# A decoder layer on one core: matmul operands read from two halves in turn, results taken out of PSUM in token order

## The chip, the cores and the metric

The kernel runs on one core of a Trainium2 chip. A core has five engines with their own instruction streams. TensorE (PE in the profile; its weight loads are PEld) multiplies matrices and writes to PSUM. VectorE (DVE), ScalarE (ACT) and GpSimd (POOL) do elementwise work. SyncE (SP) issues the DMAs. Operands lie in SBUF, 128 partitions side by side; a tile here is 128 partitions by up to 1024 float32 values.

The metric is the device time in microseconds (us) of one execution. A profile is one execution, recorded by the hardware profiler.

## The reference

One layer of a hybrid decoder, 1024 tokens of width 1024, float32:

```python
z = rms_norm(h, norm_mix_g); proj = z @ w_in                  # 1024 -> 1536
y_pool = multiscale_pool_mixer(proj[..., :512], ...)          # windows 2, 4, 8, 16, then 4 blocks of 128x128
xb = causal_depthwise_conv(proj[..., 512:1024], ...)          # 4 taps
y_lru = rg_lru(xb, gates ...) * gelu(proj[..., 1024:])        # sigmoid gates (64x64 blocks), linear recurrence
h = h + concat(y_pool, y_lru) @ w_out
z = rms_norm(h, norm_mlp_g)
h = h + square(relu(z @ w_up)) @ w_down                       # 1024 -> 4096 -> 1024
z = rms_norm(h, norm_ple_g)
h = h + sigmoid(z @ w_ple_gate + b) * (p @ w_ple_proj)
out = rms_norm(h, norm_final_g)
```

## The kernel before

**Layout.** Everything is held with the features on the partitions and the tokens along the free dimension: `H[0..7]` are eight tiles of 128 features by 1024 tokens. `T` are six work tiles, `R` holds 1/rms for each token. A matmul takes a 128x128 block of weights as the stationary operand and streams up to 512 tokens (columns) of a tile as the moving operand. Its result, 128 features by 512 tokens, fills one PSUM bank.

**Precision.** Each product of two float32 values is made of three products of rounded values (the type float32r). `split` (lines 151 to 159) writes hi, the rounded copy, on ScalarE, and lo, the rest, on VectorE. `mm` (lines 311 to 329) multiplies hi by hi, hi by lo and lo by hi into the same bank; line 321 issues nearly all matmuls of the program. `lru_gates` issues its own (line 523), two of 64 rows side by side. The sums of squares for the norms multiply by a tile of ones: lines 385 and 386 with float32r operands, line 395 with plain float32. Ten matmuls on a tile of ones (line 428) stand ahead of the first data.

**Stages**, in the order of the program:

- the first projection (`ps_l`), three output tiles accumulated while the eight tiles of x arrive and are split;
- the other projections (`ps_i`, `project`), with convolution, pooling windows, gates (`ps_g`, sigmoid on ScalarE, line 531), pool products (`ps_p`, line 591) and scans between them; `normed` (line 488) multiplies each result by R as it takes it out of PSUM;
- the output projection (`ps_o`), added to `H` on line 632;
- the up product (`ps_P_u`). Tokens and features are cut into halves, and each 2x2 block product is computed with seven products instead of eight (`P1` to `P7`, a Strassen-Winograd scheme), 16 pairs of output tiles. `copy` (line 704, ScalarE) and `add` (line 672, VectorE) take each product out of PSUM and combine it. `P5` is added to both rows of a pair through `twice`. `finish_up` then does relu, R and square, and the result goes to DRAM;
- the down product (`ps_P_d`), the same scheme over two chunks of the hidden features, accumulated in `H` (line 672 again);
- the per-layer gate (`ps_e` and `ps_j`) in three token groups, 512, 256 and 256 (`GROUPS`). `ple_out` (lines 953 to 968) takes the gate out of PSUM on line 959 or 957 and the projection on line 965;
- the final norm, with the stores.

**What sets the order.** A scheduling layer orders the instructions of each engine by readiness and priority from the order in which the code issues them; `pin` and `tc.keep_in_program_order` hold some in place. PSUM has eight banks: four single ones (`pd`) and two tiles of two banks (`pp`). `psum` and `mlp_bank` hand them out in turn. A product can start when its bank has been emptied and its operands are split.

What a result in PSUM looks like in the kernel before: column n of the bank is token n of the half. All readers take it in one run of 512 (or 1024, or 256).

Of the kernel before, what the change touches and what calls it, by code (L numbers as in the profile page):

```python
# [9 lines left out]
AF = mybir.ActivationFunctionType  # L10
ALU = mybir.AluOpType

P = 128
# [3 lines left out]
HALF = 512  # L17
# [34 lines left out]
def block_kernel(  # L52
# [85 lines left out]

    def f32(ap):
        return ap.bitcast(F32)  # L140

    def col(name, i):
        c = COLS[name] + i
        return vecs[:, c : c + 1]
# [166 lines left out]
    def mm(parts, whi, wlo, zhi, zlo, first, last, only=None, more=False, held=False):  # L311
        outs = [
            (slice(hs.start + n, hs.start + min(n + HALF, w)), ps[:, n : min(n + HALF, w)])
            for hs, ps in parts
            for w in (hs.stop - hs.start,)
            for n in range(0, w, HALF)
            if only is None or hs.start + n == only.start
        ]
        for w, z in ((whi, zhi), (whi, zlo), (wlo, zhi)):
            for hs, ps in outs:  # L320
                ins = nc.tensor.matmul(  # L321
                    ps, w, z[:, hs],
                    start=first and z is zhi and w is whi,
                    stop=last and w is wlo,
                    skip_group_check=more,
                )
                if held:
                    tc.keep_in_program_order(ins)
                    held = False
# [155 lines left out]

    def normed(dst, parts):
        for hs, ps in parts:
            nc.vector.tensor_tensor(dst[:, hs], ps, R[:, hs], ALU.mult)

    def conv(o, ps):  # L490
        u, xb = (H[6], T[4])[o % 2], H[o]
# [17 lines left out]
    def lru_gates(o):  # L509


        hi, lo = hl(0), hl(2)
        ct, rt, _ = LSETS[o % 2]
        zhi, zlo = B[4 + o]
        ps = [psum(f"ps_g{h}{o}") for h in range(2)]
        halves = [
            [(hs.start + n, x[:, n : n + HALF]) for hs, x in parts for n in range(0, hs.stop - hs.start, HALF)]
            for parts in ps
        ]
        for n, (w, z) in enumerate(((hi, zhi), (hi, zlo), (lo, zhi))):  # L520
# [12 lines left out]
        return last.ins  # L533

# [48 lines left out]
    def pool_mix(pair):  # L583
        whi, wlo = hl(1), hl(3)
        for t in range(2):
            g = 2 * pair + t
            y = (T[5], T[2])[t]
            ps = psum(f"ps_p{g}")
            mm(ps, kblk(whi, g), kblk(wlo, g), *B[g], True, True)
            for hs, part in ps:  # L590
                nc.scalar.activation(
                    y[:, hs], part, AF.Identity, bias=pool_bs[:, g : g + 1], scale=col("pool_s", g)
                )
            split(y, *B[g])

# [75 lines left out]
    def add(to, x, y=None, eng=None):  # L671
        (eng or nc.vector).tensor_tensor(to, to if y is None else y, x, ALU.add)  # L672

    def twice(x):
        return x.unsqueeze(1).broadcast_to([P, 2, x.shape[-1]])

# [42 lines left out]
    def up_first():  # L719
        cc, c11, c12, c21, c22, s = up_sums(0)  # L720
        ps = {}
        ws = {}
        for kinds in (("P6", "P7"), ("P4", "P5")):
            for kind, w in zip(kinds, weights()):
                ws[kind] = w
                ps[kind] = mlp_bank(f"ps_{kind}_u0")
                product(ps[kind], w, lambda t, kind=kind: up_operand(kind, t), range(3))
        for kind in ("P6", "P7", "P4", "P5"):
            product(ps[kind], ws[kind], lambda t, kind=kind: up_operand(kind, t), range(3, 4))
        copy(s, ps["P5"])  # L730
# [9 lines left out]
        add(c12, ps["P6"], c11)  # L740
        add(c22, ps["P7"], c12)
        add(c11, ps["P2"])
        add(c21, ps["P4"], c22)
        add(c22, s)
        add(c12, ps["P5"])
        norm.rstd(R, parts)
        done.append((0, cc))

    def up_pair(m):
        cc, c11, c12, c21, c22, s = up_sums(m)  # L750

        def of(kind, w):
            ps = mlp_bank(f"ps_{kind}_u{m}")
            product(ps, w, lambda t: up_operand(kind, t))
            return ps
# [2 lines left out]
        if m == NPAIR - 1:  # L758
            preload_down()
        copy(s, of("P1", wa))  # L760
        add(c11, of("P2", wb), s)
        if m > 1:
            store_up = finish_up(*done.pop())
            if m < NPAIR - 1:
# [2 lines left out]
            leave("hl")  # L767
        wa, wb = weights()
        copy(c12, of("P3", wb))
        add(s, of("P6", wa))  # L770
# [4 lines left out]
        add(c22, of("P7", wa), s)  # L775
        if m == NPAIR - 1:
            ask()
            prepare(0, 0)
        add(c21, of("P4", wb), c22)
        if m == 1:  # L780
            finish_up(*done.pop())()
        wa, _ = weights()
# [55 lines left out]
    def down(n):  # L838
# [6 lines left out]
        for q in range(NQ):  # L845
# [17 lines left out]
                    load_w(0, ij, i)  # L863
            if kind == "P1":
                copy(u, x)
                add(c11, x)
            elif kind == "P2":
                add(c11, x)
            elif kind == "P6":
                add(u, x)  # L870
                add(c12, u, eng=None)
            elif kind == "P7":
                add(u, x)
                add(H[2 * q + 1].rearrange("p (y s) -> p y s", y=2), twice(u))
            elif kind == "P4":
                add(c21, x)
            elif kind == "P5":
                add(h_all[:, 2 * q : 2 * q + 2, SECOND], twice(x))
            else:
                add(c12, x)  # L880
            for tp in AHEAD[q] if n else AHEAD[q - 1]:
                prepare(n + 1, tp)
            if last:
# [69 lines left out]
    def ple_out(hs, o, pg, pj, add=True, then=None):  # L953
        t = T[3 + o % 2][:, : hs.stop - hs.start]
        hv = H[o][:, hs]
        if hs == GROUPS[-1]:
            pin(nc.scalar.activation(t, pg, AF.Sigmoid, bias=col("b_ple", o)))
# [172 lines left out]
```

## Time and profile before

| | us |
|---|---|
| median of 3 runs | 972.97 (972.44 to 973.43) |
| the profiled execution | 972.32 |
| its span, first to last instruction | 970.4 |
| TensorE busy | 960.2 |
| VectorE busy | 747.2 |
| ScalarE busy | 459.1 |
| GpSimd busy | 99.1 |

The granted clock of TensorE was 0.997 of full on the mean. How to read the views quoted below: a group of instructions is one row, with line, engine, operation, what it writes and reads by the program's names, shapes and count, then busy us, the mean ns of one, and the idle time of the engine before them with what ended it. Matmuls are pipelined: a record begins when the columns start to stream and ends when the last result is out, so records overlap, and the pace is read from start to start. A mean that is marked with other forms mixes shapes. "L321" is line 321 of the kernel; after the change the same statement stands on line 336.

### The profile page before, as it was taken

The page shows a single profiled execution, that of the slowest core. Times are in us where ns is not written, and L with a number is a line of the kernel's source. Part 1 is how long each engine was busy: PE and PEld are TensorE (multiplying, and loading weights), DVE is VectorE, ACT ScalarE, POOL GpSimd, SP SyncE. Part 2 cuts the span into 40 slices and gives each one's busy share as a digit, 9 for nine tenths or more (in the row PEclk, how much of TensorE's full clock was granted, in tenths as well). Part 3 has the DMA queues.
Part 4 walks back from the last instruction along what each step waited for, and adds up shares of the span by engine and source line. Part 5 has one row for each costly group of instructions (what it writes and reads, how often), then busy time and mean ns, then how long its engine had stood idle before and what let it go on. Part 6 is the DMA issues. An engine that isn't in the chain of part 4 may idle for free.

```text
span 970.4 us, 11500 instructions
## 1 busy us (share of the span) xinstructions
PE 960.2 (99%) x4472; PEld 800.1 (82%) x4472; DVE 747.2 (77%) x865; ACT 459.1 (47%) x546; POOL 99.1 (10%) x72
## 2 busy tenths in 40 slices
PE   9999999999999999999999999999999999999996
PEld 7888788888788888888888888888888888888996
DVE  7997965459887777777677889879675669784976
ACT  8368793347443343334334535443443346552635
POOL 0000000002523322322331000000000000000220
PEclk9999999999999999999999999999999999999998
DMA  7311133112154345344434997356532341031122
GB/s 254 95 44 44 46 130 129 44 43 72 59 169 168 120 162 193 123 133 167 179 119 141 325 367 253 109 190 208 179 105 87 109 152 44 10 122 44 44 88 87
DMA packets 45190, 125.04 MB, mean 129 GB/s; under 512 B 4176, under 2 KB 6224, under 8 KB 45136
## 3 DMA queue, kind: packets, MB, share of 16 engines
q1 hardware_dynamic: 44992, 124.27, 37.9%
q8 instruction: 35, 0.57, 0.2%
q14 instruction: 19, 0.16, 0.0%
q10 hardware_dynamic: 144, 0.04, 0.0%
HBM read 90.74 MB, written 33.55 MB: 128 GB/s over the span
## 4 chain that ended last, share of the span: by engine, by line
PE 95%; DVE 3%; ACT 1%; DMA 0%; issue 0%; SPq 0%; DVEq 0%
PE ps_P_d L321 31%; PE ps_P_u L321 31%; PE ps_i L321 10%; PE ps_o L321 9%; PE ps_e L321 8%; PE ps_l L321 3%; PE ps_j L321 1%; PE ps_g L523 1%; PE ps_p L321 1%; DVE h L981 1%; DMA h<-in_xT 0%; DVE a L155 0%; DVE a L158 0%; DVE t L997 0%; DVE wu_lo L155 0%
## 5 line engine op out<-in xcount | busy, mean ns | idle before, releaser
L321 PE MATMUL ps_P_d<-a,wd_P_hi 128*128 128x512 f32 x880 | 270.8, 389 | 0.0
L321 PEld LDWEIGHTS ps_P_d<-a,wd_P_hi 128*128 128x128 f32 x880 | 165.2, 188 | 34.3
L321 PE MATMUL ps_P_d<-a,wd_P_lo 128*128 128x512 f32 x440 | 171.2, 389 | 0.0
L321 PE MATMUL ps_P_u<-a,wu_hi 128*128 128x512 f32 x512 | 157.7, 389 | 0.0
L321 PE MATMUL ps_P_u<-y,wu_hi 128*128 128x512 f32 x384 | 118.1, 389 | 0.0
L321 PEld LDWEIGHTS ps_P_u<-a,wu_hi 128*128 128x128 f32 x512 | 96.1, 188 | 20.1
L321 PE MATMUL ps_P_u<-a,wu_lo 128*128 128x512 f32 x256 | 99.6, 389 | 0.0
L672 DVE TENSOR_TENSOR t<-t,ps_P_u 128x512 f32<-128x512 f32 (+1 forms) x80 | 62.6, 784 | 47.3 <-PE ps_P_u L321 47.1
L321 PEld LDWEIGHTS ps_P_d<-a,wd_P_lo 128*128 128x128 f32 x440 | 82.6, 188 | 17.2
L321 PEld LDWEIGHTS ps_P_u<-y,wu_hi 128*128 128x128 f32 x384 | 72.1, 188 | 15.0
L321 PE MATMUL ps_i<-a,wi_hi 128*128 128x512 f32 x288 | 77.5, 391 | 0.0
L321 PE MATMUL ps_P_u<-y,wu_lo 128*128 128x512 f32 x192 | 74.8, 390 | 0.4 <-DVE wu_lo L155 0.4
L155 DVE TENSOR_TENSOR a<-wd,a 128x1024 fp32r<-128x1024 f32 x56 | 67.1, 1219 | 4.5 <-ACT a L154 3.5
L154 ACT ACTIVATE a<-wd 128x1024 fp32r<-128x1024 f32 x56 | 58.9, 1057 | 22.3 <-DMA wd<-act 12.0
L321 PE MATMUL ps_o<-y,wo_hi 128*128 128x512 f32 x256 | 68.4, 389 | 0.0
L321 PEld LDWEIGHTS ps_i<-a,wi_hi 128*128 128x128 f32 x288 | 53.7, 188 | 12.4 <-issue 1.4
L154 ACT ACTIVATE wu_hi<-wu 128x1024 fp32r<-128x1024 f32 x24 | 25.5, 1063 | 78.2 <-PE ps_P_u L321 43.9
L154 ACT ACTIVATE wu_hi<-wu_raw 128x1024 fp32r<-128x1024 f32 (+1 forms) x25 | 25.3, 1011 | 78.0 <-PE ps_P_u L321 44.5
L321 PEld LDWEIGHTS ps_o<-y,wo_hi 128*128 128x128 f32 x256 | 48.0, 188 | 10.0
L321 PEld LDWEIGHTS ps_P_u<-a,wu_lo 128*128 128x128 f32 x256 | 48.0, 188 | 9.9
L154 ACT ACTIVATE wd_P_hi<-wd 128x1024 fp32r<-128x1024 f32 x24 | 25.4, 1060 | 56.5 <-PE ps_P_d L321 51.9
L155 POOL TENSOR_TENSOR wg_lo<-wg_raw,wg_hi 128x1024 fp32r<-128x1024 f32 x4 | 9.9, 2478 | 408.0 <-DVE h L966 381.4
(224 smaller groups left out, 1628.7 us busy)
## 6 DMA issues: line engine op xcount, KB each, us to landing
wd<-act SPq DMA_DIRECT2D x56, 512.0 KB, 5.5
act<-t SPq DMA_DIRECT2D x32, 512.0 KB, 4.6
wu_raw<-in_w_up SPq DMA_DIRECT2D x16, 512.0 KB, 3.2
wu<-in_w_up SPq DMA_DIRECT2D x16, 512.0 KB, 4.1
act<-wu SPq DMA_DIRECT2D x16, 512.0 KB, 5.1
wd<-in_w_down SPq DMA_DIRECT2D x16, 512.0 KB, 6.4
h<-in_xT SPq DMA_DIRECT2D x15, 512.0 KB, 4.5
wg_raw<-in_w_gate SPq DMA_DIRECT2D x12, 512.0 KB, 3.4
```

The costliest lines, as they stand in the source:

```text
L154: first = pin(nc.scalar.activation(hi, src, AF.Copy))
L155: pin((eng or nc.vector).tensor_tensor(lo, src, f32(hi), ALU.subtract))
L321: ins = nc.tensor.matmul(ps, w, z[:, hs], start=first and z is zhi and w is whi, stop=last and w is wlo, skip_group_check=more,)
L523: nc.tensor.matmul(x, w[r, o * P : (o + 1) * P], z[r, at : at + HALF], start=n == 0, stop=n == 2)
L672: (eng or nc.vector).tensor_tensor(to, to if y is None else y, x, ALU.add)
L981: nc.vector.scalar_tensor_tensor(hv, hv, col("g_fin", o), rfin[:, hs], ALU.mult, ALU.mult)
```

## The change

Three helpers are added. `turns(z)` reads a moving operand of 512 columns as 0, 256, 1, 257, ..., 255, 511 (one of 256 as 0, 128, 1, 129, ...). The bank is still written in one run, so its column 2j holds token j of the half and column 2j + 1 token j + 256. `got(ps)` reads a bank so that the tokens come out in order: 256 values with a step of two, then the 256 between them; of a tile of two banks it does so bank by bank. `by(x, ps)` gives a tile in SBUF the same shape, which leaves its addresses in one run.

All products on lines 321 and 523 read through `turns`. All readers of their banks use `got` and `by`: `normed`, the sigmoids of `lru_gates`, `pool_mix`, the residual add of the output projection, `copy`, the adds of the up and down products (`add_got`, and `add_both` for `P5`), and `ple_out`. The matmuls on a tile of ones (lines 385, 386, 395 and 428) and what reads their banks stay as they were. Weights, splits, DMAs and the arithmetic are untouched.

On every engine the instructions stand in the same order, with the same buffers, as before; only the access patterns of operands differ.

```diff
+    def turns(z):
+        return z.rearrange("p (a j) -> p j a", a=2)
+
+    def got(ps):
+        if ps.shape[-1] > HALF:
+            return ps.rearrange("p (b j a) -> p b a j", b=2, a=2)
+        return ps.rearrange("p (j a) -> p a j", a=2)
+
+    def by(x, ps):
+        if ps.shape[-1] > HALF:
+            return x.rearrange("p (b a j) -> p b a j", b=2, a=2)
+        return x.rearrange("p (a j) -> p a j", a=2)
...
                 ins = nc.tensor.matmul(
-                    ps, w, z[:, hs],
+                    ps, w, turns(z[:, hs]),
...
     def normed(dst, parts):
         for hs, ps in parts:
-            nc.vector.tensor_tensor(dst[:, hs], ps, R[:, hs], ALU.mult)
+            nc.vector.tensor_tensor(by(dst[:, hs], ps), got(ps), by(R[:, hs], ps), ALU.mult)
...
-                        x, w[r, o * P : (o + 1) * P], z[r, at : at + HALF], start=n == 0, stop=n == 2
+                        x, w[r, o * P : (o + 1) * P], turns(z[r, at : at + HALF]), start=n == 0, stop=n == 2
...
-                        last = nc.scalar.activation(dst[HEADS[h], hs], part[r], AF.Sigmoid, bias=col(b, o)[r])
+                        last = nc.scalar.activation(
+                            by(dst[HEADS[h], hs], part), got(part[r]), AF.Sigmoid, bias=col(b, o)[r]
+                        )
...
-            nc.vector.tensor_tensor(H[o][:, hs], H[o][:, hs], part, ALU.add)
+            hv = by(H[o][:, hs], part)
+            nc.vector.tensor_tensor(hv, hv, got(part), ALU.add)
...
+    def add_got(to, ps, y=None):
+
+        add(by(to, ps), got(ps), None if y is None else by(y, ps))
+
+    def add_both(to, ps):
+
+        to = to.rearrange("p c (a j) -> p c a j", a=2)
+        add(to, got(ps).unsqueeze(1).broadcast_to([P, 2, 2, ps.shape[-1] // 2]))
...
-    def copy(to, x):
-        nc.scalar.activation(to, x, AF.Copy)
+    def copy(to, ps):
+        nc.scalar.activation(by(to, ps), got(ps), AF.Copy)
...
-        add(c11, of("P2", wb), s)
+        add_got(c11, of("P2", wb), s)
...
-        add(cc[:, :, SECOND], twice(p5))
+        add_both(cc[:, :, SECOND], p5)
...
-            nc.vector.tensor_tensor(t, pg, R[:, hs], ALU.mult)
+            nc.vector.tensor_tensor(by(t, pg), got(pg), by(R[:, hs], pg), ALU.mult)
...
-        nc.vector.tensor_tensor(e, t, pj, ALU.mult)
+        nc.vector.tensor_tensor(by(e, pj), by(t, pj), got(pj), ALU.mult)
```

More of the change, by code (lines that the diff above doesn't have):

```diff
@@ L591, in pool_mix @@
                 nc.scalar.activation(
-                    y[:, hs], part, AF.Identity, bias=pool_bs[:, g : g + 1], scale=col("pool_s", g)
+                    by(y[:, hs], part), got(part), AF.Identity, bias=pool_bs[:, g : g + 1], scale=col("pool_s", g)
                 )
@@ L739, in up_first @@
         copy(c11, ps["P1"])
[L740 to L743, printed above, removed]
+        add_got(c12, ps["P6"], c11)
+        add_got(c22, ps["P7"], c12)
+        add_got(c11, ps["P2"])
+        add_got(c21, ps["P4"], c22)
         add(c22, s)
-        add(c12, ps["P5"])
+        add_got(c12, ps["P5"])
         norm.rstd(R, parts)
@@ L769, in up_pair @@
         copy(c12, of("P3", wb))
-        add(s, of("P6", wa))
+        add_got(s, of("P6", wa))
         wa, wb = weights()
@@ L774, in up_pair @@
                 store_up()
-        add(c22, of("P7", wa), s)
+        add_got(c22, of("P7", wa), s)
         if m == NPAIR - 1:
@@ L778, in up_pair @@
             prepare(0, 0)
-        add(c21, of("P4", wb), c22)
+        add_got(c21, of("P4", wb), c22)
         if m == 1:
@@ L865, in down @@
                 copy(u, x)
-                add(c11, x)
+                add_got(c11, x)
             elif kind == "P2":
-                add(c11, x)
+                add_got(c11, x)
             elif kind == "P6":
-                add(u, x)
-                add(c12, u, eng=None)
+                add_got(u, x)
+                add(c12, u)
             elif kind == "P7":
-                add(u, x)
+                add_got(u, x)
                 add(H[2 * q + 1].rearrange("p (y s) -> p y s", y=2), twice(u))
             elif kind == "P4":
-                add(c21, x)
+                add_got(c21, x)
             elif kind == "P5":
-                add(h_all[:, 2 * q : 2 * q + 2, SECOND], twice(x))
+                add_both(h_all[:, 2 * q : 2 * q + 2, SECOND], x)
             else:
-                add(c12, x)
+                add_got(c12, x)
             for tp in AHEAD[q] if n else AHEAD[q - 1]:
@@ L956, in ple_out @@
         if hs == GROUPS[-1]:
-            pin(nc.scalar.activation(t, pg, AF.Sigmoid, bias=col("b_ple", o)))
+            pin(nc.scalar.activation(by(t, pg), got(pg), AF.Sigmoid, bias=col("b_ple", o)))
         else:
-            nc.vector.tensor_tensor(t, pg, R[:, hs], ALU.mult)
+            nc.vector.tensor_tensor(by(t, pg), got(pg), by(R[:, hs], pg), ALU.mult)
             nc.scalar.activation(t, t, AF.Sigmoid, bias=col("b_ple", o))
```

## The prediction

> **What bounds the kernel now.** I read the page's busy times first, then the chain that ended last, then busy time by stage, then single matmuls in the timeline.
>
> ```profile
> span 970.4 us, 11500 instructions
> PE 960.2 (99%) x4472; PEld 800.1 (82%) x4472; DVE 747.2 (77%) x865; ACT 459.1 (47%) x546; POOL 99.1 (10%) x72
> PE 95%; DVE 3%; ACT 1%; DMA 0%; issue 0%; SPq 0%; DVEq 0%
> ```
>
> TensorE is busy in 960.2 of 970.4 us and holds 95% of the chain. Nothing but its own pace, and the few places where it waits, can move the end. The stages, cut by hand at the borders that the chain of waits shows (the columns are the stretch and its length, then busy us and instructions of PE, PEld, DVE, ACT and POOL, the granted clock, the DMA share and GB/s):
>
> ```profile
> 1.31:5.72 4.41, 4.41 (x11) 3.46 (x11) 1.41 (x6) 2.58 (x5) 0.00 (x0) 1.00 0.71 213
> 5.72:36.00 30.28, 29.98 (x132) 24.24 (x131) 26.86 (x55) 20.42 (x25) 0.00 (x0) 1.00 0.62 214
> 36.00:150.00 114.00, 114.00 (x521) 92.26 (x520) 97.82 (x102) 85.49 (x89) 0.00 (x0) 1.00 0.21 70
> 150.75:237.79 87.04, 87.04 (x385) 72.07 (x385) 54.12 (x61) 39.03 (x43) 5.68 (x3) 1.00 0.19 61
> 237.79:258.50 20.71, 20.26 (x89) 16.43 (x89) 19.85 (x24) 11.18 (x16) 7.83 (x4) 1.00 0.29 102
> 258.51:544.35 285.84, 285.84 (x1261) 236.37 (x1261) 215.89 (x216) 106.55 (x126) 75.50 (x58) 1.00 0.45 154
> 544.35:849.00 304.65, 304.65 (x1346) 252.23 (x1345) 242.44 (x247) 137.91 (x152) 0.00 (x0) 1.00 0.48 161
> 849.00:905.10 56.10, 56.10 (x253) 46.51 (x252) 38.40 (x59) 24.57 (x36) 0.00 (x0) 1.00 0.22 72
> 905.10:929.37 24.27, 24.12 (x206) 23.74 (x205) 22.39 (x41) 11.81 (x20) 5.04 (x2) 1.00 0.27 91
> 929.37:960.94 31.57, 31.57 (x274) 31.51 (x274) 21.96 (x49) 16.84 (x34) 4.87 (x2) 1.00 0.19 65
> ```
>
> From 36 us to the end of the products TensorE hardly waits at all, at a full granted clock. So the question is what one matmul costs there. Three pieces of the timeline (start, length of the piece, count; each piece overlaps the next, since a record goes on until its results are out):
>
> ```profile
> 599.96 0.61 PE L321 MATMUL ps_P_d<-a,wd_P_hi 128*128 128x512 f32 x2
> 600.41 0.39 PE L321 MATMUL ps_P_d<-a,wd_P_lo 128*128 128x512 f32 x1
> 600.64 0.61 PE L321 MATMUL ps_P_d<-a,wd_P_hi 128*128 128x512 f32 x2
> ...
> 905.18 0.28 PE L321 MATMUL ps_e<-a,wg_lo 128*128 128x256 f32 x1
> 905.30 0.39 PE L321 MATMUL ps_e<-a,wg_hi 128*128 128x256 f32 x2
> 905.52 0.28 PE L321 MATMUL ps_e<-a,wg_lo 128*128 128x256 f32 x1
> ...
> 960.69 1.02 PE L395 MATMUL n_ps<-t,ones 128*128 128x256 f32 x4
> ```
> ```profile
> L395 PE MATMUL n_ps<-t,ones x6: 377/379/483, 960.7 to 962.7; 128*128 128x256 f32 x6
> ```
>
> Three products of 512 columns start in 0.68 us (599.96 to 600.64), 226.7 ns each. Three of 256 take 0.34 us (905.18 to 905.52), 113.3 ns each. The cost is proportional to the columns, with nothing fixed in it: 0.443 ns a column. The four records of line 395 are different. Their operand is plain float32, not the rounded kind, and it passes the array more slowly: less the length of the last record (379 ns), 1.02 us hold three starts, 214 ns for 256 columns, 0.836 ns a column. If a plain column takes two ticks of the array where a rounded one takes one (my reading; no row says it), a rounded product of 512 columns has 512 ticks too and would need the same 214 ns. It takes 226.7. So 12.7 ns in 226.7, 5.6%, are lost by something that only the faster stream meets. The loss grows with the columns read and not with the number of instructions; the reading of the operand is the candidate, and that is what the change touches.
>
> **The change part by part.** *The products.* No instruction is added, removed or moved on any engine. Each product of line 321 and line 523 reads column 0, 256, 1, 257 and so on, in place of 0, 1, 2. Its price is not in the trace, so it is bounded. Best: the loss goes, 214 ns for 512 columns, 107 for 256. The nine stages from 5.72 to 960.94 hold 953.6 us of busy TensorE (29.98 + 114.00 + 87.04 + 20.26 + 285.84 + 304.65 + 56.10 + 24.12 + 31.57); 5.6% of that is 53.4 us. Worst: every column costs a fetch of its own. The slowest pace of a 512-column product in the trace is that of the first ten:
>
> ```profile
> 1.91 1.05 PE L428 MATMUL ps_l<-ones 128*128 128x512 f32 x2
> ...
> L428 PE MATMUL ps_l<-ones x10: 561/628/792, 1.3 to 5.3; 128*128 128x512 f32 x10
> ```
>
> The two start 1.05 - 0.63 = 0.42 us apart, 1.85 times 226.7, which on 953.6 us is +811 us. I take the best end. Two streams, each in order, ask each half for a column only every second tick; where one stream at full pace falls 1 in 18 short, two at half pace leave slack. Nothing in the trace shows that two can be fed at once, and so the worst end keeps a chance below.
>
> The Trainium skill ("TensorE: Matmul & The Clock Gate", Back-to-back issue gap) gives columns / 2.4 + 2.5 ns for a warm matmul: 215.8 ns for 512 columns, 109.2 for 256. The row of line 395 agrees within its 10 ns rounding, but the 113.3 against 226.7 of the rounded products shows no fixed part. By the skill the gain would be 10.9 ns in 226.7 and 4.1 in 113.3, about 45 us.
>
> *Taking results out.* Every read of PSUM now takes each second value, in two runs, and writes in order. The values per instruction are the same. Rows of PSUM readers, of contiguous work at other lengths, and of the only reads with a step:
>
> ```profile
> L672 DVE TENSOR_TENSOR t<-t,ps_P_u 128x512 f32<-128x512 f32 x65 | 44.3, 683 | 39.4 <-PE ps_P_u L321 39.2
> L672 DVE TENSOR_TENSOR h<-h,ps_P_d 128x512 f32<-128x512 f32 x32 | 21.8, 681 | 23.4 <-PE ps_P_d L321 23.4
> L672 DVE TENSOR_TENSOR t<-t,ps_P_u 128x1024 f32<-128x1024 f32 x15 | 18.3, 1220 | 7.8 <-PE ps_P_u L321 7.8
> L672 DVE TENSOR_TENSOR h<-h,ps_P_d 128x1024 f32<-128x1024 f32 x8 | 9.7, 1215 | 0.2 <-PE ps_P_d L321 0.2
> L672 DVE TENSOR_TENSOR t<-t,ps_P_d 128x512 f32<-128x512 f32 x16 | 11.0, 685 | 22.0 <-PE ps_P_d L321 22.0
> L552 DVE TENSOR_TENSOR_SCAN h<-h 128x1024 f32<-128x1024 f32 x2 | 4.6, 2291 | 0.0
> ```
> ```profile
> L154 ACT ACTIVATE wu_hi<-wu 128x1024 fp32r<-128x1024 f32 x24 | 25.5, 1063 | 78.2 <-PE ps_P_u L321 43.9 <-POOL wu L191 32.8 <-DVE t L672 1.4
> L154 ACT ACTIVATE wu_hi<-t 128x512 fp32r<-128x512 f32 x15 | 9.5, 631 | 19.0 <-PE ps_P_u L321 19.0
> L407 ACT ACTIVATE edge<-rstd,eps 128x16 f32<-128x16 f32 x6 | 1.7, 316 | 0.0
> L407 ACT ACTIVATE edge<-t,eps 128x8 f32<-128x8 f32 x2 | 0.6, 306 | 0.3 <-DVE t L403 0.3
> ```
>
> Below, the step costs nothing (no gain, since an element already takes (1220 - 683) / 512 = 1.05 ns and no row of VectorE has one cheaper). Above, an element takes twice that, as in the scan (2291 against 1220 for 1024): +0.54 us on 512 columns. Line 407 reads every 32nd value on ScalarE: 16 against 8 values cost 316 - 306 = 10 ns, 1.25 ns each, where contiguous work costs (1063 - 631) / 512 = 0.84, half as much again. I take that half, +0.27 us per 512 on VectorE, since it is the only row with a step. Who covers it: in the up stage (258.51) that is 65 x 0.27 + 15 x 0.54 = 25.7 us on VectorE's 215.9, 242 where TensorE's new time is 285.8 x 0.944 = 270; in the down stage 48 x 0.27 + 8 x 0.54 = 17.3 on 242.4, 260 of 288. From 36 to 150 us some 24 halves of 512 (the projections' results) give 6.5 on 97.8, 104 of 107.6. Covered on the mean, barely in that last stage. ScalarE, 47% busy, covers its copies everywhere. What is late next where the cover is thin: the bank that VectorE has not emptied, and the product that wants it.
>
> *Where the faster pace is given back.* (a) 5.72 to 36: the blocks of x arrive and are split there, and in its second half ScalarE is full; the stage keeps its length: 5.6% of 29.98, 1.7 us. (b) 905.10 to 929.37: there the chain runs over VectorE and ScalarE, busy 22.39 and 11.81 us in turn: 1.4 us kept. (c) Three slices where VectorE has no idle time left:
>
> ```profile
> 48.50:72.75 24.25, 24.25 (x113) 19.55 (x112) 24.03 (x25) 14.74 (x16) 0.00 (x0) 1.00 0.13 44
> 654.75:679.00 24.25, 24.25 (x108) 20.08 (x108) 24.06 (x22) 8.62 (x9) 0.00 (x0) 1.00 0.64 209
> 800.25:824.50 24.25, 24.25 (x109) 20.08 (x108) 24.21 (x28) 16.96 (x23) 0.00 (x0) 1.00 0.14 44
> ```
>
> Each gives back its 1.4, 4.1 us together. (d) The stepped reads there and between 36 and 150 us: an estimate of 4 us, 5 or 6 reads in each slice at 0.27 with about half of it waited for. (e) After the last product two reads of 256, 0.2 us. Sum 11.4.
>
> **The sum.** The profiled execution took 972.32 us, 1.9 outside its span, and lies 0.65 under the median of 972.97. 972.3 - 53.4 + 11.4 = 930.3, or 931 against the median. By the skill's gap alone it would be 972.3 - 45 + 11.4 = 939.
>
> **The rivals.** *The reading is slower (the other side).* A hop at every column may cost instead of help. Line 407 speaks for it: with a step, an element costs 1.25 ns in place of 0.84. It decides at once: TensorE has no idle time, so every ns over 226.7 per product adds about 4 us. At half as much again the products take 340 ns, +477 us: 1450 us; at the pace of the first ten, 1784. Against it: those first ten are the start of the program, and line 407 reads 8 or 16 values, mostly fixed cost.
>
> The Trainium skill ("Advanced Engine Details and Errata", SBUF Cachelines) says that full pace needs at least two hits in a row on a 16-byte line, and a new line at each access is penalised. By that rule this rival is right, since consecutive columns here lie 1 KB apart; no run so far shows it for TensorE.
>
> *The pace stays.* The 5.6% may be the array's own in this number format, and 226.7 stays. Then only the stepped reads are left, nearly all under cover: 973 with free ones, up to 980 with (c), (d) and the stage from 36 us paying for theirs. For it: the loss is the same to the nanosecond in all stages, whatever the other engines and DMA do. Against it: it is a loss per column, not per product.
>
> *The pace is gained but VectorE gives it back.* At the upper price, +0.54 us per 512, the up stage needs 215.9 + 65 x 0.54 + 15 x 1.08 = 267 of 270 us, the stage from 36 us 111 of 108. Local queues would eat some half of the gain: 950 to 965.
>
> **How the numbers follow.** Forecast (pace gained, mostly covered) 0.62, its own range 918 (free steps, nothing given back but (a)) to 950. VectorE gives back half: 0.06. Pace stays: 0.13. Slower reading: 0.19. The range 917 to 982 holds the first three, 0.81. What this kernel's measurement can tell from no change is about 0.2%, 2 us. Faster: 0.62 + 0.06 = 0.68. The pace-stays case splits in 0.08 within and 0.05 over. Slower: 0.19 + 0.05 = 0.24.
>
> **What would show it.** In the timeline of the changed kernel, three 512-column products in 0.64 to 0.65 us in place of 0.68 prove the gain, 0.68 the stay, anything above the loss. The 683 ns group of VectorE shows the step's price: 683 is free, near 950 is my value, 1220 the upper one. TensorE's busy share below 97% in a stage shows where it is given back; from 36 to 150 us and 800 to 825 us I expect VectorE as the releaser. I am wrong if the pace of line 395 is not what the array gives a rounded operand.

## The result, and the profile after

| | before | after |
|---|---|---|
| median, us | 972.89 (972.44 to 973.43, 4 runs) | 945.35 (943.47 to 946.44, 4 runs) |
| profiled execution, us | 972.32 | 946.09 |
| its span, us | 970.4 | 944.3 |

The ratio is 0.9715, with a 95% interval of 0.9697 to 0.9733: 27.5 us faster. The forecast was 931 in a range of 917 to 982. The sign came out, and the faster products are where the gain comes from; the size did not: 42 us were forecast.

The page of the changed kernel, its span, busy times and chain:

```profile
span 944.3 us, 11521 instructions
PE 923.0 (98%) x4472; PEld 804.5 (85%) x4472; DVE 747.8 (79%) x865; ACT 456.9 (48%) x546; POOL 99.0 (10%) x72
PE 69%; DVE 17%; ACT 5%; DMA 4%; issue 3%; POOL 1%; SPq 0%; DVEq 0%; ACTq 0%; POOLq 0%
```

TensorE is busy 37 us less, VectorE and ScalarE the same. The chain has changed: VectorE now holds 17% of it and not 3%, DMA 4% and not 0. There are 21 more instructions, and none is work: the counts of the engines are those of before, and in the trace the 21 are instructions that only wait (event semaphores). So the text ahead of the prediction was wrong in one point: not the access patterns alone differ, but some waits too, and one of these matters (below).

The pace, in the timeline of the changed kernel (start, length of the piece, count). The first two rows are the first and last of a stretch without a wait, with 95 products of 512 columns between the two starts; the next two are the same for 81 products of 256 columns:

```profile
639.73 0.38 PE L336 MATMUL ps_P_d<-a,wd_P_hi 128*128 128x512 f32 x1
...
660.24 0.38 PE L336 MATMUL ps_P_d<-a,wd_P_hi 128*128 128x512 f32 x1
...
905.81 0.39 PE L336 MATMUL ps_e<-a,wg_hi 128*128 128x256 f32 x2
...
914.86 0.39 PE L336 MATMUL ps_e<-a 128*128 128x256 f32 x2
```

20.51 us for 95 is 215.9 ns in place of 226.7; 9.05 us for 81 is 111.7. Over the 1077 products from 596.78 to 829.23 us the pace is 215.8, so a product of 512 columns gains 10.9 ns. At 256 columns the three starts of the prediction (113.3 ns) were too few. Before, over the first 66 products of these groups, the timeline has

```profile
904.23 0.88 PE L321 MATMUL ps_j<-proj,proj 128*128 128x256 f32 x6
...
911.82 0.40 PE L321 MATMUL ps_e<-a 128*128 128x256 f32 x2
```

which is 7.59 us for 66, 115.0 ns each: a product of 256 columns gains 3.3. The step on the taking side, in the groups of VectorE and ScalarE by form (mean ns of one behind the comma); the last row is ScalarE's before:

```profile
L690 DVE TENSOR_TENSOR t<-t,ps_P_u 128x512 f32<-128x512 f32 x65 | 44.3, 683 | 26.0 <-PE ps_P_u L336 25.7
L731 ACT ACTIVATE t<-ps_P_u 128x512 f32<-128x512 f32 x32 | 18.5, 579 | 0.6 <-PE ps_P_u L336 0.5
L704 ACT ACTIVATE t<-ps_P_u 128x512 f32<-128x512 f32 x32 | 18.6, 580 | 0.8 <-PE ps_P_u L321 0.8
```

683 and 579 ns, where before it was 683 and 580. Reading every second value of a bank costs nothing in the duration.

The stages are cut at the first start of each one's products (`ps_l`, `ps_i`, `ps_o`, `ps_P_u`, `ps_P_d`, and the gate in its first group `ps_e` and its two groups of 256). Busy time in four of them, `ps_o`, up, down and the two groups of 256; the columns are those of the prediction's table:

```profile
145.66:234.69 89.03, 86.08 (x385) 74.61 (x384) 56.72 (x63) 40.09 (x45) 4.89 (x3) 0.96 0.20 64
234.69:529.83 295.14, 292.71 (x1349) 254.15 (x1348) 237.36 (x240) 116.56 (x141) 84.05 (x61) 1.00 0.45 155
529.83:824.05 294.22, 291.41 (x1345) 253.48 (x1344) 243.13 (x247) 137.55 (x152) 0.00 (x0) 1.00 0.50 167
876.79:936.92 60.13, 56.98 (x491) 55.18 (x489) 46.70 (x95) 31.75 (x60) 9.82 (x4) 1.00 0.21 71
```

Against the kernel before, cut at the same products. "Possible" is the stage's products times 10.9 ns, or times 3.3 ns for the last row:

| stage | products | before, us | after, us | possible | gained | lost |
|---|---|---|---|---|---|---|
| `ps_l` | 144 | 34.27 | 33.81 | 1.6 | 0.5 | 1.1 |
| `ps_i` and mixing | 480 | 110.60 | 106.25 | 5.2 | 4.4 | 0.9 |
| `ps_o` | 384 | 87.04 | 89.03 | 4.2 | -2.0 | 6.2 |
| up | 1344 | 306.56 | 295.14 | 14.6 | 11.4 | 3.2 |
| down | 1344 | 304.65 | 294.22 | 14.6 | 10.4 | 4.2 |
| gate, 512 | 240 | 55.39 | 52.74 | 2.6 | 2.7 | 0 |
| gate, 2 x 256 | 480 | 58.81 | 60.13 | 1.6 | -1.3 | 2.9 |
| sum | | 957.3 | 931.3 | 44.4 | 26.0 | 18.4 |

The pace alone was worth 44.4 us; 18.4 of that was given back, a third of it in the output projection, which became longer. What TensorE waits for, by instruction (us in total, times, longest). In the kernel before the same view had, beside the start's 1.3, only 0.6, 0.4, 0.3 and 0.2:

```profile
PE ps_o L336 <- DVE wo_lo L170: 3.0, 1, 3.0
PE ps_P_u L336 <- DVE wu_lo L170: 2.1, 2, 1.6
PE ps_e L336 <- DVE t L992: 2.0, 1, 2.0
PE ps_P_d L336 <- DVE wd_P_lo L170: 1.9, 3, 0.8
```

The rows of `ps_o`, `ps_P_u` and `ps_P_d` are splits: VectorE makes the low half of an operand (line 170) later than the faster TensorE wants it. Of these four only the `ps_e` row is a bank that was not emptied in time.

The longest, at the start of the output projection, in the timeline (in brackets the idle time before, and what ended it):

```profile
145.66 1.03 PE L336 MATMUL ps_o<-y,wo_hi 128*128 128x512 f32 x4
149.64 1.22 PE L336 MATMUL ps_o<-y,wo_lo 128*128 128x512 f32 x2 [2.96 <-DVE wo_lo L170]
150.66 1.91 PE L336 MATMUL ps_o<-y,wo_hi 128*128 128x512 f32 x4
152.36 1.06 PE L336 MATMUL ps_o<-y,wo_lo 128*128 128x512 f32 x2
...
155.70 0.59 PE L336 MATMUL ps_o<-y,wo_hi 128*128 128x512 f32 x2
```

Four products run, then TensorE waits 2.96 us for the low half of the first output weights. After the wait four products take 150.66 to 152.36 = 1.70 us, 425 ns each, half the pace, and so it goes on almost to 155.70: the 14 products from 149.64 need 6.06 us, where 14 x 0.216 is 3.02. The stage's granted clock is 0.96, and 0.50 in the 6.8 us from 148.78 to 155.61; every other stage has 1.00. The wait and these 3.0 us are 6.0 of the stage's 6.2.

The last stage's wait, at the first group of 256, begins on ScalarE. Its rows there after and, below, before:

```profile
901.66 1.28 ACT L987 ACT_TABLE_LOAD   x1 [6.75 <-DVE t L986]
902.96 0.91 ACT L987 ACTIVATE t<-t,vecs 128x256 f32<-128x256 f32 x2
```
```profile
921.67 1.28 ACT L960 ACT_TABLE_LOAD   x1
928.36 0.91 ACT L960 ACTIVATE t<-t,vecs 128x256 f32<-128x256 f32 x2 [5.40 <-DVE t L959]
```

Before, the load of the sigmoid's table ran at once (921.67) and the sigmoid alone waited for VectorE. After, the load itself waits, and its 1.28 us stand between VectorE's result and the sigmoid. What line 987 has on ScalarE's queue in this stretch (ACTq; 901 to 904.6 us) says why:

```profile
L987 ACTq EVENT_SEMAPHORE  x2: 17/17/17, 901.6 to 901.9; - x2
```

These instructions only wait, here for VectorE's semaphore, and the first of the two stands at 901.6, right ahead of the load at 901.66. Before, line 960 has none of them: the two sigmoids wait for VectorE themselves, behind the load. After, the sigmoids (line 987, unchanged in the diff) wait on ScalarE's own semaphore, and their wait for VectorE stands in instructions of its own, one of them ahead of the load. The product of the next tile wants the bank that line 992 empties behind this sigmoid, and waits 2.0 us for it.

Where the prediction had expected the loss, in the VectorE-full slices, there is none. The two slices moved to where the same work now stands, then one at the start of the down stage that the prediction did not look at:

```profile
637.20:660.80 23.60, 23.60 (x111) 20.68 (x110) 23.57 (x22) 10.68 (x11) 0.00 (x0) 1.00 0.61 203
778.80:802.40 23.60, 23.60 (x111) 20.68 (x110) 23.60 (x27) 16.76 (x23) 0.00 (x0) 1.00 0.14 45
542.80:566.40 23.60, 23.05 (x107) 19.89 (x106) 21.58 (x23) 9.99 (x12) 0.00 (x0) 1.00 1.00 368
```

In the first two VectorE is busy 23.57 and 23.60 of 23.60 us, and TensorE does not wait: 109 products start in each, as many as 23.6 us hold at 216 ns. The slice from 48.50 of the prediction now lies near 47.00 to 70.30; there too VectorE and TensorE are both busy in all of the 23.30 us. In the third row the DMA share is 1.00 (368 GB/s), and the chain of waits of the changed kernel runs over transfers there (start, us):

```profile
547.89 6.41 DMA wd<-in_w_down
554.31 9.24 DMA wu<-in_w_down
```

Just behind the border of the up and the down stage the queue is full. It was as full there before (1.01, 376 GB/s, from 557.60 to 581.60 us): the transfers have not changed, the products come sooner. The operands arrive late for them, and so their splits; that a faster transfer would end these waits was not tried.

### The profile page after: what moved, and what is told of

It reads as the page before. It is cut to its first block, busy times and chain, and to the rows that moved or that the text cites. A ratio compares the mean times of both kernels' runs of the same rounds, so it can differ in the third digit from the quotient of the medians.

```text
span 944.3 us, 11521 instructions
## 1 busy us (share of the span) xinstructions
PE 923.0 (98%) x4472; PEld 804.5 (85%) x4472; DVE 747.8 (79%) x865; ACT 456.9 (48%) x546; POOL 99.0 (10%) x72
## 4 chain that ended last, share of the span: by engine, by line
PE 69%; DVE 17%; ACT 5%; DMA 4%; issue 3%; POOL 1%; SPq 0%; DVEq 0%; ACTq 0%; POOLq 0%
PE ps_P_u L336 26%; PE ps_P_d L336 24%; PE ps_o L336 8%; PE ps_e L336 7%; PE ps_l L336 2%; DVE h L512 2%; DVE a L170 1%; DVE y L170 1%; DVE t L503 1%; DMA wu<-in_w_down 1%; PE ps_j L336 1%; DMA act<-t 1%; DVE wi_lo L170 1%; DVE y L173 1%; DVE wu_lo L170 1%
## 5 line engine op out<-in xcount | busy, mean ns | idle before, releaser
L336 PE MATMUL ps_P_d<-a,wd_P_hi 128*128 128x512 f32 x880 | 261.7, 379 | 0.0
L336 PE MATMUL ps_P_d<-a,wd_P_lo 128*128 128x512 f32 x440 | 167.1, 380 | 1.9 <-DVE wd_P_lo L170 1.9
L336 PE MATMUL ps_P_u<-a,wu_hi 128*128 128x512 f32 x512 | 152.5, 379 | 0.2 <-DVE a L170 0.2
L336 PE MATMUL ps_P_u<-y,wu_hi 128*128 128x512 f32 x384 | 114.1, 379 | 0.1
L336 PE MATMUL ps_P_u<-a,wu_lo 128*128 128x512 f32 x256 | 97.0, 379 | 0.0
L336 PE MATMUL ps_i<-a,wi_hi 128*128 128x512 f32 x288 | 74.3, 381 | 0.0
```

Source lines behind the costliest of these rows:

```text
L336: ins = nc.tensor.matmul(ps, w, turns(z[:, hs]), start=first and z is zhi and w is whi, stop=last and w is wlo, skip_group_check=more,)
```

## The experiments

**1. One part each.** Kernel one has only the product's side of the change (`turns`), with the readers of before. Kernel two has only the reader's side; its products read in one run. The results of both have their tokens in another place, as their expectations say.

```diff
e1_read_only, against before:
-                    ps, w, z[:, hs],
+                    ps, w, turns(z[:, hs]),
...
e2_take_only, against after:
     def turns(z):
-        return z.rearrange("p (a j) -> p j a", a=2)
+        return z
```

> The kernel before with the stepped reading of the operands alone; results are taken out of PSUM in one run as before, so the tokens of each half are left in the wrong order in the output. Theory A (all of the gain is the pace of the products, and the stepped taking out of PSUM is free): 226.7 ns per 512-column product becomes 216 as in the changed kernel, and the time is that of the changed kernel, 943 to 948 us. Rival (the stepped taking costs VectorE time that shows at the borders of the stages): below 940 us.

Measured: 941.46 us (940.78 to 943.83), ratio 0.9678 (0.9662 to 0.9693), between the two ranges of the expectation. The faster reading is the whole gain, and without the other half of the change it is worth 3.9 us more than with it. TensorE's waits:

```profile
PE ps_o L324 <- DVE wo_lo L158: 3.0, 1, 3.0
...
PE ps_e L324 <- DVE t L968: 0.5, 1, 0.5
```

The wait for the late split is here too; it belongs to the pace. That for `ps_e` has shrunk to 0.5.

> The changed kernel with the operands read in order as before; results are still taken out with a step of two, so the tokens of each half are left in the wrong order in the output. Theory A (the stepped taking is free): 973 us within 2, VectorE's 512-value group on PSUM at 683 ns. Rival (it costs something the group's duration does not show): 976 us or more.

Measured: 974.78 us (974.17 to 976.42), ratio 1.0018 (1.0008 to 1.0027): 1.6 us over the kernel before on the same chip. Its groups and waits:

```profile
L690 DVE TENSOR_TENSOR t<-t,ps_P_u 128x512 f32<-128x512 f32 x65 | 44.4, 684 | 39.8 <-PE ps_P_u L336 39.5 <-ACT t L731 0.2
```
```profile
PE ps_e L336 <- DVE t L992: 1.7, 1, 1.7
```

684 ns: the step is free here as well. The wait of the late table load is there, and about as long as the whole excess of 1.6. In the two traces the last stage is 1.8 us longer than before, and the down stage 0.8, where a split comes late. What the reader's side costs is waits, not a duration.

**2. Which order of columns.** Four kernels change only the order in which a product reads its 512 columns; each has one profiled execution. A letter in an expectation is a theory, and stands there with what it says.

```diff
e3_evens_odds: 0, 2, 4, ... 510, then 1, 3, 5, ...
+        return z.rearrange("p (j a) -> p a j", a=2)
e4_pairs: 0, 1, 256, 257, 2, 3, 258, 259, ...
+        return z.rearrange("p (a j b) -> p j a b", a=2, b=2)
e5_near16: 0, 4, 1, 5, 2, 6, 3, 7, then 8, 12, ...
+        return z.rearrange("p (b a j) -> p b j a", a=2, j=4)
e6_near64: 0, 16, 1, 17, ... 15, 31, then 32, 48, ...
+        return z.rearrange("p (b a j) -> p b j a", a=2, j=16)
```

> The changed kernel, but each product reads columns 0, 2, 4, ... 510 and then 1, 3, ... 511 (one stream with a step of two); the output has its tokens in another order than it should. Theory N (the loss comes from two successive columns that are neighbours in memory): no two successive columns are neighbours, so the pace is 216 ns and the time about 945 us. Theory P (the next piece of a contiguous stream is not there in time; two streams at half pace give it time): one stream that uses up its memory twice as fast loses more, 240 ns per product, some 1000 us or more.

> The changed kernel, but each product reads two neighbours from the one half, then two from the other: 0, 1, 256, 257, 2, 3, 258, 259 and so on; the output has its tokens in another order than it should. Theory N (neighbours one after the other are the loss): half or all of the loss is back, 221 to 227 ns per product, 957 to 973 us. Theory P (two streams at half pace give the next piece time): 216 ns, about 945 us.

Measured: 1914.51 and 1433.79 us. The pace, in the timeline of evens and odds, then of pairs (where a row is left out, here and below, it holds one product):

```profile
699.58 1.08 PE L336 MATMUL ps_P_u<-y,wu_hi 128*128 128x512 f32 x2
...
700.94 0.63 PE L336 MATMUL ps_P_u<-y,wu_hi 128*128 128x512 f32 x1
```
```profile
699.57 0.85 PE L336 MATMUL ps_P_u<-y,wu_hi 128*128 128x512 f32 x2
700.25 0.51 PE L336 MATMUL ps_P_u<-y,wu_lo 128*128 128x512 f32 x1
```

Three products in 1.36 us, 453 ns each; two in 0.68, 340 ns. Neither theory of these two expectations had both numbers: the order with every second column is exactly twice the pace of one run (2 x 226.7), and pairs are one and a half times it. Both fell. The theory that took their place (L) counts fetches of 16 bytes, four columns. By it the columns are handed in turn to two sides, the even places of the stream to one and the odd places to the other; a side fetches again whenever its next column lies in another 16 bytes than its last; a fetch takes 1.77 ns, which is 226.7 divided by 128. One run makes 128 fetches a side: 128 x 1.77 = 226.7. Evens and odds make 256: 453. The two halves in turn make 64 a side, 113 ns, less than the 216 that was measured, so something else sets the pace there. Pairs would make 256 and take 453; they took 340, so the theory missed one of its four orders from the start. The next runs put it to the test.

> The changed kernel, but each product reads two streams that lie 16 bytes apart: columns 0, 4, 1, 5, 2, 6, 3, 7, then 8, 12 and so on; the output has its tokens in another order than it should. Theory L (columns in even and in odd places are fed apart, each side keeps the last 16 bytes that it fetched, and a fetch takes 2.125 ticks of 0.83 ns: 1 fetch in 2 columns of a side in order gives 226.7 ns, 1 in 1 gives 453 as with evens then odds, 1 in 4 gives the array's own 216): each side uses its 16 bytes fully, 216 ns, about 945 us. Rival F (the two streams have to lie far apart): 227 ns or more, 973 us or more. If the piece kept is 32 bytes or longer, 227 ns as well.

> The changed kernel, but each product reads two streams that lie 64 bytes apart: columns 0, 16, 1, 17, ... 15, 31, then 32, 48 and so on; the output has its tokens in another order than it should. Theory L: 216 ns, about 945 us, and so with kept pieces of 32 or 64 bytes. Rival F (far apart): 227 ns or more.

Measured: 944.64 and 943.89 us, as the changed kernel. The timeline of the first:

```profile
700.23 0.59 PE L336 MATMUL ps_P_d<-a,wd_P_hi 128*128 128x512 f32 x2
...
700.88 0.38 PE L336 MATMUL ps_P_d<-a,wd_P_hi 128*128 128x512 f32 x1
```

Three in 0.65 us, 216 ns. The distance between the two streams does not matter down to 16 bytes: theory F, by which they must lie far apart, is out.

**3. More and fewer streams.** Two more orders, one profiled execution each:

```diff
e7_quarters: 0, 128, 256, 384, 1, 129, ...
+        return z.rearrange("p (a j) -> p j a", a=4)
e8_swap: 0, 2, 1, 3, 4, 6, 5, 7, ...
+        return z.rearrange("p (j b a) -> p j a b", a=2, b=2)
```

> The changed kernel, but each product reads from four quarters in turn: columns 0, 128, 256, 384, 1, 129 and so on; the output has its tokens in another order than it should. Theory L: each side goes between two streams, so nearly every column needs a fetch: 340 ns (as with pairs) to 453 ns (as with evens then odds), 1440 to 1920 us. Rival F (streams that lie far apart, any number of them): 216 ns, about 945 us.

> The changed kernel, but each product reads columns 0, 2, 1, 3, 4, 6, 5, 7 and so on; the output has its tokens in another order than it should. Theory L with kept pieces of 16 bytes: each side takes two columns from each piece, as in plain order, 227 ns, about 973 us. If the piece is 8 bytes: 216 ns. If neighbours in a row were the loss: 216 ns.

Measured: 1205.72 and 975.33 us. The timelines, quarters first:

```profile
699.77 0.73 PE L336 MATMUL ps_P_d<-a,wd_P_hi 128*128 128x512 f32 x2
...
700.62 0.73 PE L336 MATMUL ps_P_d<-a,wd_P_hi 128*128 128x512 f32 x2
```
```profile
699.74 0.61 PE L336 MATMUL ps_P_d<-a,wd_P_hi 128*128 128x512 f32 x2
...
700.42 0.61 PE L336 MATMUL ps_P_d<-a,wd_P_hi 128*128 128x512 f32 x2
```

The swap inside a group of four takes 0.68 us for three, 226.7 ns, the pace of one run, as theory L says: only one column in four there comes right behind its lower neighbour (4 behind 3), yet the whole loss stays, since both sides touch all 128 groups. Quarters take 0.85 us for three, 283 ns, and that theory L missed: a side that goes to and fro between two streams should fetch at every column. In units of 1.77 ns, evens and odds are 256, pairs 192, quarters 160, one run and the swap 128. The count of two sides explains the orders in which a side reads one stream (five: one run, halves, near, swap, evens and odds), not those in which it reads two (pairs, quarters). What a side keeps then is open, and with it whether two sides are the right picture at all.

**4. The waits behind the change.** The changed kernel was timed again, beside three mends. The first gives the sigmoid of line 987 the same view of its tile that line 986 writes, so that the framework sees one shape and not two:

```diff
e10_sigmoid_view, against after:
-            nc.scalar.activation(t, t, AF.Sigmoid, bias=col("b_ple", o))
+            nc.scalar.activation(by(t, pg), by(t, pg), AF.Sigmoid, bias=col("b_ple", o))
e11_view_and_wo_early, against e10:
-    todo += [(load_weights, w_out[o], f"wo{o}") for o in range(NT)]
+    todo += [(load_weights, w_out[o], f"wo{o}", S, None, nc.sync, URGENT * (o < 1)) for o in range(NT)]
e12_gate_split_dve, against e10:
-            (load_weights, w_gate[o], f"wg{g}_{o}", S, nc.gpsimd if g else None) for o in os
+            (load_weights, w_gate[o], f"wg{g}_{o}", S, None) for o in os
```

> The changed kernel once more, as the reference for the two that follow: 943 to 947 us.

Measured: 944.96 us (942.84 to 945.74), ratio 0.9708 (0.9693 to 0.9722). The profiled execution, 942.84, shows the start of the output projection again, timeline and stage:

```profile
149.03 0.70 PE L336 MATMUL ps_o<-y,wo_lo 128*128 128x512 f32 x2 [2.95 <-DVE wo_lo L170]
149.56 1.03 PE L336 MATMUL ps_o<-y,wo_hi 128*128 128x512 f32 x4
```
```profile
145.05:231.89 86.84, 83.41 (x385) 72.41 (x384) 56.71 (x63) 40.11 (x45) 5.74 (x3) 1.00 0.19 65
```

The same wait, but no half pace behind it (two products in 0.53 us, and the four that follow take the 1.03 us of the four ahead of the wait in the first trace), and the stage is 2.2 us shorter. So the wait is the kernel's, and the drop of the clock is not in every execution of it. Eight traces with the faster pace show this place. From 140 to 165 us the granted clock is 1.00 in three of them (this one, `e5_near16`, `e10_sigmoid_view`), 0.93 in four (`e1_read_only`, `e6_near64`, `e11_view_and_wo_early`, `e12_gate_split_dve`) and 0.86 in the first trace of the changed kernel: half the clock for no time, for 3.4 us or for 6.8. The stage is 86.8 us long without it, 87.8 to 88.6 with the short one, 89.0 with the long one. All eight have a wait of 2.9 to 3.0 us ahead of it; what decides is not shown. Nor can it be all of the 3 us over which the times of this kernel spread: of the four executions here, those of 942.84 and 945.74 us both have a mean clock of 0.998.

> The changed kernel with the sigmoid of the first two token groups written and read through the same two-run view as the multiplication before it; the arithmetic is the same. Theory W (the mixed views made the framework put a wait on ScalarE's table load, so that it follows VectorE's long row in place of running beside it): the load runs ahead again, the 2.27 us gap of TensorE near 902 us shrinks by 1.5 to 1.9 us, and the time is 2 us below the changed kernel, 942 to 944. Rival (taking results out with a step is slow in itself in this stage): no difference within 1 us.

Measured: 941.31 us (940.55 to 943.72), ratio 0.9678 (0.9664 to 0.9693), 3.7 us under the changed kernel on the same chip and the best median of this study with the tokens in order. ScalarE's timeline and TensorE's wait:

```profile
891.21 1.28 ACT L987 ACT_TABLE_LOAD   x1
897.89 0.91 ACT L987 ACTIVATE t<-t,vecs 128x256 f32<-128x256 f32 x2 [5.40 <-DVE t L986]
```
```profile
PE ps_e L336 <- DVE t L992: 0.6, 1, 0.6
```

The load runs ahead again, the wait falls from 2.0 to 0.6 us, and the last stage from 60.13 to 58.05. The median is that of the product's side alone (941.46): with this one line mended, taking the results out in order costs nothing that can be measured. The stage shows 2.1 of the 3.7 us; the rest is not located, and the two intervals only just touch. The two executions with a trace, neither with a drop of the clock, are 1.6 us apart (942.84 and 941.23).

> As the kernel before it, and the split of the first block of the output projection's weights gets a higher priority, so that VectorE does it ahead of one split and two other operations; the arithmetic is the same. Theory C (the 3.3 us that TensorE waits for this split near 146 us cost twice: the wait, and 13 products at half pace behind it because the clock falls): wait and slow products go, the output projection's stage takes 83 to 85 us in place of 89, and the time is 4 to 6 us below the kernel before it, 937 to 940. Rival (another operand of the same stage is late too): the wait moves to the next product and 1 to 2 us are gained.

Measured: 943.91 us (943.41 to 944.21), ratio 0.9699 (0.9683 to 0.9715): no gain over 0.9678, and neither of the expected times. The wait has changed its name:

```profile
PE ps_o L336 <- ACT y L169: 2.9, 1, 2.9
```

The weights are split early now, and the mixers' result is late by as much, 8 us further on (at 157.87 us). In both orders VectorE and ScalarE owe TensorE some 3 us of work here. That theory C had the price of the wait right is not shown by this run, since the wait stayed.

> The kernel with the sigmoid's view, and the rounding rests of the gate weights of the second and third token groups are made by VectorE instead of GpSimd (four operations of 1024 values); the arithmetic is the same. Theory G (in the second token group VectorE and ScalarE set the pace, and two rows of VectorE that are 0.41 and 0.47 us long elsewhere take 2.17 and 2.59 us there while GpSimd works): the rows go back to 0.4 to 0.5 us, VectorE gains 2 x 1.22 us of work, 1.4 us are saved on the chain, and the time is 939 to 941 us, 0.9660 of the kernel before. Rival (the products of that stage set the pace): no difference within 1 us, 0.9678.

Measured: 941.67 us (940.83 to 942.38), ratio 0.9676 (0.966 to 0.9692). Its two-group stage took 56.65 us where the first mend's took 58.05, as expected. What was removed is seen in the first mend's timeline, GpSimd and then VectorE:

```profile
878.49 2.58 POOL L170 TENSOR_TENSOR wg_lo<-wg_raw,wg_hi 128x1024 fp32r<-128x1024 f32 x1 [366.64 <-ACT wg_hi L169]
```
```profile
879.18 2.17 DVE L170 TENSOR_TENSOR a<-t,a 128x256 fp32r<-128x256 f32 x1
...
886.72 0.41 DVE L170 TENSOR_TENSOR a<-t,a 128x256 fp32r<-128x256 f32 x1
```

The same operation of VectorE takes 2.17 us while GpSimd's split is under way and 0.41 when GpSimd is idle. Not every operation is slowed: one that reads an operand from PSUM (line 992, at 878.85) took 0.42 us in the same time. Without GpSimd's splits the stage is 1.4 us shorter, but the totals cannot be told apart: inconclusive for the time.

## Why the prediction was right, and where it was not

**Right.** TensorE's pace bounded the kernel, and the loss lay in how the columns are read: products went from 226.7 to 215.9 ns, and the readers' step cost nothing. The three products in "0.64 to 0.65 us" that were to prove it are there (600.02 to 600.67). Two rivals, the slower reading and the pace that stays, fell with it, and the one in which VectorE gives half back by a dear step fell at 683 ns.

**Right for a reason that did not hold.** That two streams have slack because each is asked only every second tick would give the pairs the same slack: they are two such streams as well, and took 340 ns. Four streams are asked still less often, and took 283. With no row for the price of the hop, "I take the best end" was a choice between two bounds, and that the best one came is in part luck.

**The price of the best pace.** The step "214 ns for 512 columns, 107 for 256" was too good. The products then took 215.9, which changes 5.6% to 4.8%, and at 256 columns 111.7. The first came from four records of line 395, whose length is given to 10 ns, some 3 ns for each of the three starts. The second came from "nothing fixed in it", read from three products: over 66 it was 115.0 and not 113.3. Possible were 44.4 us, not 53.4. That is 9.0 of the miss of 16, from the 930.3 us that were forecast for the profiled execution to 946.09. At 256 columns the weight loads are busy 55.18 of TensorE's 56.98 us; that they set the 111.7 was not tried.

The Trainium skill ("TensorE: Matmul & The Clock Gate", Back-to-back issue gap) gave 215.8 for 512 columns, and the trace agrees to a tenth of a ns; for 256 it gave 109.2, and the trace does not, with 111.7. The sum by it, 45 us of gain, was the better of the two terms: 44.4 were possible.

**What is given back.** The sum was 11.4 and came out as 18.4, 7.0 of the miss, and its parts were mostly elsewhere:

- (a) `ps_l` keeps its length: forecast 1.7, measured 1.1. Right.
- (b) the first part of the groups of 256: 1.4 forecast, 2.9 measured over both groups, and 2.1 of it by another mechanism than VectorE and ScalarE in turn: the late table load. After its mend the stage is 58.05, 0.8 under before, half of the possible gain.
- (c) the three VectorE-full slices, 4.1: wrong. An engine without idle time in a slice is not late if it has run ahead; in none of the three does TensorE wait.
- (d) the stepped reads, 4: wrong. They cost nothing in VectorE's time; the second experiment's excess is one of waits.
- Not in the sum at all: the wait for late splits where one stage hands over to the next. The output projection loses 6.2, the up stage 3.2, the down stage 4.2. The waits for splits, with those too short for the rows shown above, are 3.0, 2.3 and 2.8 of these; 3.0 more in the output projection is the half pace, and the product behind each wait takes 0.32 us in place of 0.22. "I expect VectorE as the releaser" was right about the engine, but the reason was the splits and not the step, and the price appears behind the borders: at 146.7 us, from 243 to 281, and from 533 to 596.

Two steps failed. One is the size of the best pace, above. The other is (c) and (d) together: the cover was judged by VectorE's mean and by its fullest slices, while what was late in these traces is the single operand that one of the next stage's early products needs. Before, `ps_o` waited for nothing. Its stage now starts 4.9 us earlier (145.66 against 150.59), and what VectorE has to do ahead of the first split stands in the same order as before.

**"No instruction is added."** The count rose by 21, and a wait moved. Equal order is not equal waits: 14 instructions on ScalarE's queue belong to line 987 and only wait, where line 960 had none, and one of them holds the table load back.

**The other rule.** The Trainium skill ("Advanced Engine Details and Errata", SBUF Cachelines) asks that subsequent accesses hit the same 16-byte line, at least twice. The runs contradict it for this operand: halves in turn never hit a line twice in a row and give 216 ns; evens and odds hit each line twice in a row and give 453. The 16 bytes themselves agree with the swap (227) and the near order (216), if the hits are counted for each side.

## What to carry to other kernels

Where the pace of float32r matmuls is some 5% over 216 ns for 512 columns, try reading the moving operand as two streams in turn; in these runs the two could lie as near as 16 bytes, and four streams, pairs or a step of two made it 25% to 100% slower than one run. Judge what a faster engine will gain behind the borders of stages, by what its early instructions there wait for, and not by the mean load of the others. When a view of a tile changes, look at the waits and not only at the order: give each reader and writer of the tile the same view, and see that a table load has no wait.

## What the runs showed of the hardware that was not expected

- The order of reading sets the pace of a float32r product of 512 columns over a factor of two: 216 ns (two streams), 226.7 (one run, or swapped inside 16 bytes), 283 (four streams), 340 (pairs of two streams), 453 (every second column).
- VectorE and ScalarE read PSUM with a step of 8 bytes at the same speed as in one run: 683 and 579 ns for 512 values.
- After a wait of 3 us TensorE ran at half pace for some 6 us in one execution (425 ns a product, clock 0.96 over the stage) and at full pace in another of the same kernel (1.00). Of eight traces with such a wait, three show no half clock, four show 3.4 us of it and one 6.8.
- VectorE's split of 256 values took 2.17 us beside a GpSimd operation, 0.41 with GpSimd idle; an operation with one operand in PSUM took 0.42 beside it.
- The product behind a wait took 0.32 us to the next start, in place of 0.22, in the output projection, the up and the down stage.
